# Small transfers and GpSimd arithmetic change places in a fused RWKV-7 and short-convolution kernel

## The chip, the cores and the metric

The kernel runs on one core of one Trainium2 chip. TensorE (PE in the rows) does the matrix products, VectorE (DVE) the elementwise arithmetic, ScalarE (ACT) activations, casts and copies, GpSimd (POOL) some elementwise work, and SyncE (SP) nothing but the start of transfers. Transfers can also be started from GpSimd's and ScalarE's queues; each of the five engines works through its instructions in the order in which they stand in its queue. The metric is the device time of one execution in microseconds (us), and the median of several runs.

## The reference

Two layers over 512 latent tokens with a prefix of 256 context tokens, 1024 channels, float32. Layer 0 is cut here to the part that the change touches; layer 1 is a Conformer convolution module.

```
r,k,v,za,bg,cg,xb,zb = split(h @ w_in)          # eight projections of 1024 channels
decay, a = low-rank maps of h (ev_w1, ev_w2; ev_a1, ev_a2), two directions z
kd  = k * (1 + (a - 1) * k_a)                   # two directions
S_t = S_{t-1}*decay + (S_{t-1} @ -kk)(kk*a)^T + v kd^T    # scan, 16 heads, both directions,
o_t = S_t @ r                                   # started from the state that the context leaves
bonus = sum(r * kd * r_k, per head) * v         # summed over both directions
ya  = head_group_norm(o) + bonus
yb  = bg * dwconv3(cg * xb)
y   = concat(ya * silu(za), yb * silu(zb)) @ w_out
```

## The kernel before, in words

**Number format.** A projection is a product of float32 values kept as two rounded parts, high and low. `hilo` (L121 to L128) loads a weight tile from memory into `wr..` (SyncE's queue), ScalarE casts it to the high part `wh..` (L126), and one engine subtracts to get the low part `wl..` (L127). Which engine subtracts is set by `lo_for` (L333): GpSimd for the tiles whose name begins with `bg` or `zb` (`POOL_SPLIT`, L30) and for `k0`, VectorE for the rest.

**Stages.** The 16 heads are worked on in 8 pairs of 128 channels. Layer 0 runs in 12 stages: 4 for the context chains (`c` at the end of a tile's name, two pairs each) and 8 for the latent chains (`l`, one pair each). In a latent stage `s` the program writes out, beside the chain of pair `s`: the triangular solve of the next pair (`solve`, L630 to L669), the loads, projections, decays and gates of the pair after that (`prep_lat`, `light`, `heavy`), the gates and the end of the pair's own output (`fills`, `finish`), and one of eight parts of the short convolution (`conv_branch`). A scheduler at build time decides in which order these stand in each engine's queue; the order is fixed when the kernel runs.

**The chain.** Each of its 8 steps passes the state `Hl` from VectorE (L757) to TensorE (`zol<-Hl`), on to ScalarE (`Ol` L744, `UV` L750), back to TensorE (`uh`) and to VectorE. It needs the solve of its own pair to be done.

**The solve.** It has 62 small dependent VectorE operations (L644 and L646, in turns), after a transpose of `Nt` into `X` (L638) and ahead of two transposes (L649 into `Nt`, L650 into `Y`). The end of L650 is called the end of the solve here, after which ScalarE copies (L655, L664, L669) and TensorE (`uh<-Yl`, `uh<-Nt`) finish the matrix `E` that the chain reads. `X`, `Y` and `Nt` have one buffer each; `Y` is filled from a constant in memory (`unit`, L637) ahead of every solve.

**Other lines that the change touches.** `light0` loads two small matrices `lwr` in four transfers on ScalarE's queue (L431), casts them (L434) and subtracts on GpSimd (L437). `heavy` forms `kd` (L518, then L520) and the bonus product `bon` on GpSimd (L524 to L527), followed on VectorE by the scaled products `al`, `AR`, `BK` (L528 to L544). `finish` loads the gate `gz` and stores to `ysp` (L797 to L801); `conv_branch` ends with `yb*gz` on GpSimd and a store to `ysp` (L836, L837). `psp` holds the shifted `k`, `v`, `r` and the gate `za` between a projection and its use; `h0d` holds the state that the context chains leave. `rest` (L857) loads the matrix `mod_w` in the first context stages on GpSimd's queue.

```
V.transpose(X..., Nt...)                                            # L638
for i in range(31, 0, -1):
    V.tensor_tensor(out=tv, in0=X[...], in1=Y[...], op=ALU.mult)    # L644
    V.tensor_tensor(out=Y[...], in0=Y[...], in1=tv, op=ALU.add)     # L646
```

## Time and profile before

| | |
|---|---|
| median of 3 runs | 1518.8 us (1510.12 to 1520.1) |
| the profiled execution | 1514.09 us |
| its span, first to last instruction | 1512.3 us |
| granted TensorE clock, mean of the span | 0.975 |
| span of six latent stages, 523.5 to 904.9 us | 381.4 us |

The span is 1.8 us shorter than the execution's own time. The stages of layer 0 lie between about 90 and 1000 us of it; what stands behind (output projection and layer 1) is not in the diff, apart from the low parts' engine being VectorE there already.

In the rows a line names the engine, the operation, `out<-in` tiles, the shape and a duration. A number in brackets, or behind the last bar, is how long the engine had been idle before the instruction, with what ended that idle time behind the arrow. "PEclk" is the granted TensorE clock as a share of full speed: 1.00 is 2.4 GHz and 0.50 is 1.2 GHz.

### The profile page before, as it was taken

Reading aid. Unit: us, or ns where it says so; the run is one execution under the profiler, and the core shown is the slowest. Engines: PE = TensorE matmul, PEld = TensorE weight load, DVE = VectorE, ACT = ScalarE, POOL = GpSimd, SP = SyncE. Lnnn points to the kernel's source line nnn. Section 1 sums busy time; section 2 is a strip of 40 time slices with the busy share of each in tenths; the row PEclk is TensorE's granted clock in tenths of the full one; section 3 lists DMA queues with packets and bytes.
Section 4 is the critical chain, followed back from the end, with each engine's and each line's share of the span. In section 5 each row is a group of like instructions: output and inputs, shape, how many; then the busy total and the mean of one; then the engine's idle time right before and its main releaser. Section 6 shows DMA issues by size and latency. Waiting matters only on the chain. (4 is left out here: it accounts for less than half of the span.)

```text
span 1512.3 us, 29639 instructions
## 1 busy us (share of the span) xinstructions
PE 1427.9 (94%) x11857; PEld 1015.2 (67%) x11857; DVE 991.9 (66%) x2202; ACT 745.3 (49%) x1512; POOL 205.4 (14%) x220
## 2 busy tenths in 40 slices
PE   5699999999999999999999999999999999999998
PEld 1374577878766666666666666677766676688876
DVE  2675597578788798987888987458545526444333
ACT  4323464375656566565556566447553314364322
POOL 0523200000020331322223130111100000000000
PEclk9799999999989999997999999999999999999999
DMA  8644533313232222211222222468503203033222
GB/s 308 172 140 166 159 111 100 93 55 96 74 107 68 77 70 70 71 59 58 64 66 73 71 57 63 148 219 288 179 20 112 94 19 112 28 108 98 90 95 84
DMA packets 146954, 156.59 MB, mean 104 GB/s; under 512 B 15266, under 2 KB 109154, under 8 KB 146816
## 3 DMA queue, kind: packets, MB, share of 16 engines
q1 hardware_dynamic: 134208, 128.76, 27.1%
q0 software_dynamic: 6928, 22.66, 4.5%
q10 hardware_dynamic: 5680, 3.29, 0.7%
q8 instruction: 93, 1.52, 0.4%
q14 instruction: 45, 0.37, 0.1%
HBM read 137.36 MB, written 17.31 MB: 102 GB/s over the span
## 5 line engine op out<-in xcount | busy, mean ns | idle before, releaser
L646 DVE TENSOR_TENSOR Yl<-Yl,xtmpl 128x126 f32<-128x126 f32 (+22 forms) x248 | 76.0, 306 | 4.1
L644 DVE TENSOR_TENSOR xtmpl<-Xl,Yl 128x126 f32<-128x126 f32 (+22 forms) x248 | 72.3, 292 | 4.1
L58 PE MATMUL pal<-ARl,BKl 64*128 64x128 f32 x512 | 60.4, 323 | 8.8 <-DVE E L589 6.5
L58 PEld LDWEIGHTS pal<-ARl,BKl 64*128 64x128 f32 x512 | 45.5, 211 | 26.7 <-issue 6.9
L58 PE MATMUL zol<-Hl,ARl 64*64 64x64 f32 x896 | 50.6, 232 | 9.4 <-DVE Hl L757 9.3
L589 DVE TENSOR_TENSOR E<-pal,maskE 128x512 f32<-128x512 f32 x64 | 42.3, 684 | 23.5 <-PE pal L58 17.6
L58 PE MATMUL zol<-UV,E 64*64 64x64 f32 (+1 forms) x1024 | 54.7, 223 | 0.4 <-ACT UV L750 0.4
L58 PEld LDWEIGHTS zol<-Hl,ARl 64*64 64x64 f32 x896 | 35.4, 134 | 29.3 <-issue 17.7
L62 PE MATMUL o<-wl,y 128*128 128x512 f32 x124 | 50.6, 408 | 4.2 <-DVE wl L127 4.2
L1092 DVE TENSOR_TENSOR a<-pu,a 128x512 f32<-128x512 f32 x16 | 11.1, 692 | 61.4 <-PE pu L63 59.1
L127 DVE TENSOR_TENSOR wl<-wr,wh 128x1024 fp32r<-128x1024 f32 x28 | 36.3, 1296 | 22.9 <-ACT wh L126 22.7
L61 PE MATMUL o<-wh,y 128*128 128x512 f32 x124 | 49.7, 400 | 0.0
L63 PE MATMUL o<-wh,y 128*128 128x512 f32 x124 | 49.6, 400 | 0.0
L750 ACT COPY UV<-uh 64x128 f32<-64x128 f32 x128 | 33.2, 259 | 32.7 <-PE uh L58 26.4
L1097 ACT CAST ah<-a 64x512 fp32r<-64x512 f32 x32 | 19.8, 618 | 56.0 <-DVE a L1092 55.5
L58 PEld LDWEIGHTS uh<-UV,BKt 128*64 128x64 f32 x704 | 26.5, 137 | 30.0 <-ACT UV L750 23.0
L437 POOL TENSOR_TENSOR lwll<-lwrl,lwhl 64x256 fp32r<-64x256 f32 x16 | 12.9, 808 | 243.8 <-PE pac L58 199.4
L58 PEld LDWEIGHTS zol<-UV,E 64*64 64x64 f32 (+1 forms) x1024 | 42.9, 138 | 3.4 <-ACT UV L750 2.2
L757 DVE SCALAR_TENSOR_TENSOR Hl<-uh,PCl,HPl 128x64 f32<-128x64 f32 x112 | 26.3, 276 | 27.4 <-PE uh L58 16.6
L58 PE MATMUL uh<-UV,BKt 128*64 128x64 f32 x704 | 36.5, 233 | 5.3 <-ACT UV L750 4.7
L126 ACT CAST wh<-wr 128x1024 fp32r<-128x1024 f32 x28 | 29.4, 1049 | 23.0 <-PE o L62 10.9
L58 PEld LDWEIGHTS uh<-Ol,E 64*64 64x64 f32 x512 | 20.1, 134 | 26.5 <-ACT Ol L744 18.5
(959 smaller groups left out, 4437.3 us busy)
## 6 DMA issues: line engine op xcount, KB each, us to landing
wr<-in_ev_w_out_dram SPq DMA_DIRECT2D x28, 512.0 KB, 4.0
mwr<-in_mod_w_dram POOLq DMA_DIRECT2D x32, 256.0 KB, 4.3
mwo<-in_mod_w_dram POOLq DMA_DIRECT2D x32, 256.0 KB, 3.1
ectx<-in_mod_w_dram SPq DMA_DIRECT2D x12, 512.0 KB, 4.5
wrk<-in_ev_w_in_dram SPq DMA_DIRECT2D x16, 256.0 KB, 3.0
wrv<-in_ev_w_in_dram SPq DMA_DIRECT2D x16, 256.0 KB, 2.9
wrr<-in_ev_w_in_dram SPq DMA_DIRECT2D x16, 256.0 KB, 3.1
wrza<-in_ev_w_in_dram SPq DMA_DIRECT2D x16, 256.0 KB, 3.0
```

Of the source, the lines that this page charges most:

```text
L58: return T.matmul(o, lhsT, rhs, start=start, stop=stop)
L61: T.matmul(o, ah, bh, start=start, stop=False)
L62: T.matmul(o, ah, bl, start=False, stop=False)
L63: T.matmul(o, al, bh, start=False, stop=stop)
L126: S.copy(hi, raw)
L127: env["lo"].tensor_tensor(out=lo, in0=raw, in1=hi, op=ALU.subtract)
L589: V.tensor_tensor(out=E[:, h, z * NLAT + c0 : z * NLAT + c0 + m, :], in0=pas[h], in1=maskE[:, z * (1 + h) : z * (1 + h) + 1, 0:x].to_broad ...
L644: V.tensor_tensor(out=tv, in0=X[:, :i, i : i + 1].to_broadcast([P, i, m]), in1=Y[:, i : i + 1, c0:].to_broadcast([P, i, m]), op=ALU.mult)
L646: V.tensor_tensor(out=Y[:, :i, c0:], in0=Y[:, :i, c0:], in1=tv, op=ALU.add)
L750: u_ = S.copy(UV[ZR[1 - h], i : 2 * nch - i : 2 * nch - 1 - 2 * i, ZR[h]], uh[ZR[1 - h], 0:2, :])
L757: h_ = V.scalar_tensor_tensor(out=Hn[:, z, :], in0=uh[:, 2 + z, :], scalar=PC[z][:, i : i + 1], in1=HP[:, z, :], op0=ALU.mult, op1=ALU.add)
L1097: S.copy(ahl[s][hr], a[hr])
```

## The change

GpSimd loses all its elementwise work in the latent stages and is given most of the small transfers. The low parts of `bg` and `zb` and of `lwr` and the product `yb*gz` go to VectorE. The bonus product goes to ScalarE for the first direction and to VectorE, as one fused operation and one product, for the second. The scaling of `kd` (L518) goes from VectorE to ScalarE, for latent and context pairs alike. Of the transfers, the stores and loads of `psp`, the loads of `h0d`, `gz` and `unit` and the stores to `ysp` go from SyncE's queue to GpSimd's, and the four `lwr` loads of each pair go from ScalarE's queue to GpSimd's. Line numbers of the changed kernel are one lower from L31 on.

```diff
-POOL_SPLIT = ("bg", "zb")
     def lo_for(nm):
-        env["lo"] = G if nm == "k0" or nm[:-1] in POOL_SPLIT else V
+        env["lo"] = G if nm == "k0" else V
...
-        nc.sync.dma_start(psp[p, which], rl)
+        nc.gpsimd.dma_start(psp[p, which], rl)
...
-            nc.sync.dma_start(t, psp[p, which])
+            nc.gpsimd.dma_start(t, psp[p, which])
-        nc.sync.dma_start(st["H"], h0d[p].rearrange("p (z x) -> p z x", z=2))
+        nc.gpsimd.dma_start(st["H"], h0d[p].rearrange("p (z x) -> p z x", z=2))
...
-                    nc.scalar.dma_start(raw[64 * b : 64 * b + 64, i], src[0, :, :, ps_].rearrange("z r c -> r z c"))
+                    nc.gpsimd.dma_start(raw[64 * b : 64 * b + 64, i], src[0, :, :, ps_].rearrange("z r c -> r z c"))
...
-                G.tensor_tensor(out=lwl[rows], in0=raw[rows, i], in1=lwh[rows, i], op=ALU.subtract)
+                V.tensor_tensor(out=lwl[rows], in0=raw[rows, i], in1=lwh[rows, i], op=ALU.subtract)
...
-            V.tensor_scalar(out=kd[:, cs], in0=a[:, cs], scalar1=hka[:, p : p + 1], scalar2=oka[:, p : p + 1],
-                            op0=ALU.mult, op1=ALU.add)
+            S.activation(kd[:, cs], a[:, cs], AF.Identity, scale=hka[:, p : p + 1], bias=oka[:, p : p + 1])
         V.tensor_tensor(out=kd, in0=kd, in1=k_, op=ALU.mult)
         if lat:
-            bt = w("tmp", "bt" + nm) if z else bon
-            G.tensor_scalar(out=bt, in0=kd, scalar1=col("r_k", 8 * z + p), scalar2=None, op0=ALU.mult)
+            rk = col("r_k", 8 * z + p)
             if z:
-                G.tensor_tensor(out=bon, in0=bon, in1=bt, op=ALU.add)
-                G.tensor_tensor(out=bon, in0=bon, in1=r_, op=ALU.mult)
+                V.scalar_tensor_tensor(out=bon, in0=kd, scalar=rk, in1=bon, op0=ALU.mult, op1=ALU.add)
+                V.tensor_tensor(out=bon, in0=bon, in1=r_, op=ALU.mult)
+            else:
+                S.activation(bon, kd, AF.Copy, scale=rk)
...
-        nc.sync.dma_start(Y, I["unit"])
+        nc.gpsimd.dma_start(Y, I["unit"])
...
-        G.tensor_tensor(out=yb, in0=yb, in1=gz, op=ALU.mult)
-        nc.sync.dma_start(ysp[8 + p], yb)
+        V.tensor_tensor(out=yb, in0=yb, in1=gz, op=ALU.mult)
+        nc.gpsimd.dma_start(ysp[8 + p], yb)
```

The loads of `gz`, the stores of `ysp` in `finish` and of the gate `za` change their queue in the same way. Queue by queue, SyncE goes from 420 to 321 entries and GpSimd from 203 to 254, of which 131 are transfers that were elsewhere before; VectorE goes from 2140 to 2183 and ScalarE stays at 1284.

The scheduler also puts VectorE's queue in another order. The first place is the end of a solve in the later latent stages of the kernel before, on VectorE; `Hl_4` and `Hl_5` are the states of the chain's fifth and sixth step, and `kd`, `P` and `BK` belong to the `heavy` of a later pair.

```order
L644 TENSOR_TENSOR xtmpl_8883<-Xl_8881,Yl_8882 128x16
L757 SCALAR_TENSOR_TENSOR Hl_4_8775<-uh_120,PCl_7420,HPl_4_8743 128x64
L757 SCALAR_TENSOR_TENSOR Hl_4_8775<-uh_120,PCl_7449,HPl_4_8743 128x64
L770 TENSOR_TENSOR Ol_8610<-zol_4_8751,Ol_8610 128x128
L646 TENSOR_TENSOR Yl_8882<-Yl_8882,xtmpl_8883 128x16
L518 TENSOR_SCALAR kdl_9109<-al_9100,hka,oka 128x512
L649 STREAM_TRANSPOSE Nt<-Yl_8882 128x32x16
L509 SCALAR_TENSOR_TENSOR Pl_9102<-scm,sg 128x528
L650 STREAM_TRANSPOSE Yl_8882<-Nt 128x512
L520 TENSOR_TENSOR kdl_9109<-kdl_9109,kl_9023 128x512
L757 SCALAR_TENSOR_TENSOR Hl_5_8810<-uh_120,PCl_7420,HPl_5_8778 128x64
```

The same engine and the same kind of place in the changed kernel; `wlcg` is the low part of a convolution weight, the three `bonl` rows are the end of a pair's output and the bonus of another, and `Hl_0` is the first state of the chain that this solve serves.

```order
L645 TENSOR_TENSOR Yl_8043<-Yl_8043,xtmpl_8044 128x2x15
L126 TENSOR_TENSOR wlcg_9269<-wrcg_9267,whcg_9268 128x512
L643 TENSOR_TENSOR xtmpl_8044<-Xl_8042,Yl_8043 128x16
L645 TENSOR_TENSOR Yl_8043<-Yl_8043,xtmpl_8044 128x16
L648 STREAM_TRANSPOSE Nt<-Yl_8043 128x32x16
L649 STREAM_TRANSPOSE Yl_8043<-Nt 128x512
L798 SCALAR_TENSOR_TENSOR bonl_6569<-po_8412,hcol,bonl_6569 128x512
L799 SCALAR_TENSOR_TENSOR bonl_6569<-bonl_6569,hcol,gz_8429 128x512
L623 SCALAR_TENSOR_TENSOR bonl_8223<-pbonl_8866,vl_8186 128x512
L637 STREAM_TRANSPOSE Xl_8869<-Nt 128x32x32
```

Before, the solve ends between two steps of the running chain, with the rows of the chain's last three steps still behind it; now it ends behind the running chain, three rows ahead of the next solve's transpose (L637 there), and its own chain begins right after it.

The second place is GpSimd's queue over about one latent stage, first of the kernel before.

```order
L524 TENSOR_SCALAR bonl_7404<-kdl_7422,cols_68 128x512
L127 TENSOR_TENSOR wlbg_7700<-wrbg_7698,whbg_7699 128x512
L524 TENSOR_SCALAR btl_7454<-kdl_7451,cols_68 128x512
L526 TENSOR_TENSOR bonl_7404<-bonl_7404,btl_7454 128x512
L527 TENSOR_TENSOR bonl_7404<-bonl_7404,rl_7369 128x512
L127 TENSOR_TENSOR wlbg_7706<-wrbg_7704,whbg_7705 128x512
L127 TENSOR_TENSOR wlzb_7738<-wrzb_7736,whzb_7737 128x512
L437 TENSOR_TENSOR lwll_8207<-lwrl_8201,lwhl_8206 64x256 x2
L127 TENSOR_TENSOR wlzb_7744<-wrzb_7742,whzb_7743 128x512
L836 TENSOR_TENSOR yb_7694<-yb_7694,gzb_7773 128x512
```

And of the changed kernel; `vl`, `kl`, `rl` are loads of `psp`, and `Yl<-in_unit` is the load that a solve starts from.

```order
L430 DMA lwrl_8191<-in_ev_w_dram 64x2x128
L430 DMA lwrl_8191<-in_ev_a_dram 64x2x128
L636 DMA Yl_8043<-in_unit_dram 128x512
L800 DMA ysp<-bonl_5742 128x512
L395 DMA vl_8186<-psp 128x512
L397 DMA h_4_7356<-h0d 128x128
L836 DMA ysp<-yb_7684 128x512
L395 DMA kl_9011<-psp 128x512
L395 DMA rl_9015<-psp 128x512
L796 DMA gz_8429<-psp 128x512
L430 DMA lwrl_9018<-in_ev_w_dram 64x2x128
```

Ten arithmetic operations of a stage are replaced by twelve transfers, in an order that repeats from stage to stage, each waiting for its own tile and all behind one another.

## Rows read from the trace of the kernel before

**Rows 1.** The profile's list of busy time by engine over the whole span: us, share of the span, number of instructions.

```profile
PE 1427.9 (94%) x11857; PEld 1015.2 (67%) x11857; DVE 991.9 (66%) x2202; ACT 745.3 (49%) x1512; POOL 205.4 (14%) x220
```

**Rows 2.** Busy time of each engine in windows of time, one window per latent stage; one of the six, and their sum and mean. Behind the window: its length, busy us (instructions) of each engine, and behind those the granted TensorE clock, the share of the transfer engines and GB/s.

```profile
647.20:712.90 65.70, 62.11 (x751) 42.74 (x751) 54.21 (x147) 36.96 (x88) 16.93 (x10) 0.84 0.21 63
...
sum 381.40, PE 359.49 PEld 247.53 DVE 325.02 ACT 227.51 POOL 96.54; mean PE 59.91 PEld 41.26 DVE 54.17 ACT 37.92 POOL 16.09
```

**Rows 3.** The same view of the windows between 444 and 741 us in which the granted clock was half; the two in the six latent stages, and the sum of all five.

```profile
689.80:710.20 20.40, 20.40 (x211) 14.81 (x213) 12.70 (x31) 9.04 (x16) 2.70 (x3) 0.50 0.17 50
734.10:741.00 6.90, 6.90 (x56) 4.35 (x55) 5.18 (x19) 3.84 (x10) 0.00 (x0) 0.51 0.00 0
sum 44.40, PE 44.40 PEld 32.47 DVE 30.62 ACT 19.88 POOL 7.11; mean PE 8.88 PEld 6.49 DVE 6.12 ACT 3.98 POOL 1.42
```

**Rows 4.** The timeline (start, duration, instruction, idle time before it) of VectorE, GpSimd and TensorE around 682 to 688 us, and the first and the last of 50 VectorE instructions between 398 and 960 us that lasted over 0.2 us longer than the median of their kind; the 50 together were 41.3 us longer.

```profile
429.31 0.58 DVE L413 SCALAR_TENSOR_TENSOR rnql<-rnql 128x16 f32<-128x16 f32 x1
...
682.49 0.24 DVE L644 TENSOR_TENSOR xtmpl<-Xl,Yl 128x78 f32<-128x78 f32 x1
682.63 1.77 DVE L542 TENSOR_TENSOR ARl<-rl,Pl 128x512 f32<-128x512 f32 x1
684.33 1.31 DVE L646 TENSOR_TENSOR Yl<-Yl,xtmpl 128x78 f32<-128x78 f32 x1
...
682.50 1.36 POOL L526 TENSOR_TENSOR bonl<-bonl,btl 128x512 f32<-128x512 f32 x1
683.93 1.61 POOL L527 TENSOR_TENSOR bonl<-bonl,rl 128x512 f32<-128x512 f32 x1
...
687.98 0.45 PE L58 MATMUL zol<-Hl,ARl 64*64 64x64 f32 x8 [2.02 <-DVE Hl L757]
...
953.62 1.77 DVE L827 SCALAR_TENSOR_TENSOR yb<-cx,hcol,yb 128x512 f32<-128x512 f32 x1
```

**Rows 5.** The timeline of VectorE at six marks of the latent stages: two ends of a solve (L650), the first and last state of the first latent chain and the first state of the second (L757), the end of a solve in a later stage, and the first state of the seventh chain.

```profile
514.58 0.71 DVE L650 STREAM_TRANSPOSE Yl<-Nt 128x512 f32<-128x512 f32 x1
533.68 0.24 DVE L757 SCALAR_TENSOR_TENSOR Hl<-uh,PCl,HPl 128x64 f32<-128x64 f32 x1
558.01 0.28 DVE L757 SCALAR_TENSOR_TENSOR Hl<-uh,PCl,HPl 128x64 f32<-128x64 f32 x1 [0.50 <-PE uh L58]
579.06 0.71 DVE L650 STREAM_TRANSPOSE Yl<-Nt 128x512 f32<-128x512 f32 x1
596.20 0.43 DVE L757 SCALAR_TENSOR_TENSOR Hl<-uh,PCl,HPl 128x64 f32<-128x64 f32 x2
...
752.11 0.70 DVE L650 STREAM_TRANSPOSE Yl<-Nt 128x512 f32<-128x512 f32 x1
...
921.28 0.47 DVE L757 SCALAR_TENSOR_TENSOR Hl<-uh,PCl,HPl 128x64 f32<-128x64 f32 x2
```

**Rows 6.** Groups of VectorE instructions by line over the whole span: count, busy us, mean ns of one, idle before. The last line is the same view of 964 to 1045 us.

```profile
L127 DVE TENSOR_TENSOR wlcg<-wrcg,whcg 128x512 fp32r<-128x512 f32 x16 | 10.9, 683 | 0.8 <-PE plr L63 0.8
L520 DVE TENSOR_TENSOR kdl<-kdl,kl 128x512 f32<-128x512 f32 x16 | 11.0, 685 | 0.0
L799 DVE SCALAR_TENSOR_TENSOR bonl<-po,hcol,bonl 128x512 f32<-128x512 f32 x8 | 6.0, 747 | 6.8 <-PE po L58 6.8
L518 DVE TENSOR_SCALAR kdl<-al,hka,oka 128x512 f32<-128x512 f32 x16 | 8.6, 540 | 0.0
L518 DVE TENSOR_SCALAR kdc<-ac,hka,oka 128x256 f32<-128x256 f32 x16 | 6.1, 404 | 1.0 <-ACT ac L505 0.9
...
L127 DVE TENSOR_TENSOR y<-yr,y 128x256 fp32r<-128x256 f32 x21 | 8.7, 419 | 0.0
```

**Rows 7.** Groups of ScalarE instructions by line over the whole span, with the columns of rows 6.

```profile
L354 ACT ACTIVATE lk<-plk,omu 128x512 f32<-128x512 f32 x8 | 5.4, 681 | 1.2 <-PE plk L63 1.2
L354 ACT ACTIVATE kc<-pck,omu 128x256 f32<-128x256 f32 x8 | 3.8, 474 | 6.0 <-PE pck L63 5.9
```

**Rows 8.** The timeline of ScalarE: one of the 32 starts of an `lwr` load in its queue (ACTq), and the cast that waits for a pair's four loads.

```profile
767.17 0.65 ACTq L431 DMA_DIRECT2D lwrl<-in_ev_a_dram  x1
...
769.63 0.62 ACT L434 CAST lwhl<-lwrl 128x512 fp32r<-128x512 f32 x1 [1.04 <-DMA lwrl<-in_ev_a_dram]
```

**Rows 9.** Groups of GpSimd instructions by line over the whole span, with the columns of rows 6.

```profile
L127 POOL TENSOR_TENSOR wlbg<-wrbg,whbg 128x512 fp32r<-128x512 f32 x16 | 24.8, 1551 | 57.4 <-ACT whbg L126 31.1 <-PE pcg L63 12.4 <-ACT HPl L721 11.8
L524 POOL TENSOR_SCALAR btl<-kdl,cols 128x512 f32<-128x512 f32 x8 | 18.0, 2253 | 41.9 <-DVE kdl L520 41.9
L437 POOL TENSOR_TENSOR lwll<-lwrl,lwhl 64x256 fp32r<-64x256 f32 x16 | 12.9, 808 | 243.8 <-PE pac L58 199.4 <-ACT lwhl L434 24.2 <-PE pvl L58 19.5
L857 POOL DMA_DIRECT2D mwr<-in_mod_w_dram x32 | 17.4, 546 | 12.3 <-PE mpb L58 11.6 <-PE uh L58 0.4 <-issue 0.3
```

**Rows 10.** The profile's list of transfers: tile, queue, count, KB of one, median us from its start to its landing.

```profile
mwr<-in_mod_w_dram POOLq DMA_DIRECT2D x32, 256.0 KB, 4.3
mwo<-in_mod_w_dram POOLq DMA_DIRECT2D x32, 256.0 KB, 3.1
Yc<-in_unit_dram SPq DMA_DIRECT2D x4, 256.0 KB, 3.4
wrk<-in_ev_w_in_dram SPq DMA_DIRECT2D x16, 256.0 KB, 3.0
```

**Rows 11.** TensorE's waits between 398 and 1000 us: who waited for whom, us in total, how often, the longest.

```profile
PE zol L58 <- DVE Hl L757: 9.3, 8, 2.0
```

More of the change, by code (lines that the diff above doesn't have):

```diff
@@ L796, in finish @@
         gz = w("tmp", f"gz{p}")
-        nc.sync.dma_start(gz, psp[p, 3])
+        nc.gpsimd.dma_start(gz, psp[p, 3])
         oT = st["bon"]
@@ L800, in finish @@
         V.scalar_tensor_tensor(out=oT, in0=oT, scalar=hc("lnx_b", p), in1=gz, op0=ALU.add, op1=ALU.mult)
-        (nc.gpsimd if p == 7 else nc.sync).dma_start(ysp[p], oT)
+        nc.gpsimd.dma_start(ysp[p], oT)
     def fill(p):
@@ L805, in fill @@
         gz = gate(p, 24, "za")
-        nc.sync.dma_start(psp[p, 3], gz)
+        nc.gpsimd.dma_start(psp[p, 3], gz)
     def after(anchor):
@@ L884, in fills @@
                 gz = gate(p, 24, "za")
-                nc.sync.dma_start(psp[p, 3], gz)
+                nc.gpsimd.dma_start(psp[p, 3], gz)
     sts = [prep_ctx(0, rest)]
```

## The prediction

> **What bounds the kernel now.** The list of busy time by engine comes first [rows 1]: TensorE works for 94% of the span, GpSimd for 14%. An average says little of the part that is changed, so the second view is the busy time by latent stage [rows 2]. Six stages take 381.4 us, 63.6 each; TensorE is busy for 59.9 of that, VectorE for 54.2, ScalarE for 37.9, GpSimd for 16.1. TensorE's 59.9 are not all needed. Five stretches between 444 and 741 us run at a granted clock of 0.50, the level of 1.2 GHz, with TensorE busy throughout [rows 3]: 44.4 us, of which full clock would have left at best 22.2. The longest, 20.4 us from 689.8, follows an idle time of TensorE of 2.02 us that a late `Hl` of the chain had caused [rows 4]; that stage shows 0.84 in rows 2. So layer 0 is bound by TensorE and VectorE together, and the places where one waits for the other cost twice where the clock then falls.
>
> The third view is the timeline around that idle time [rows 4]. VectorE's product into `AR` took 1.77 us, where the same shape takes 0.69 elsewhere [rows 6], and a solve operation 1.31 us, where its neighbour took 0.24. Both end about 0.5 us after a GpSimd operation that ran at the same time. All 50 stretched VectorE operations between 398 and 960 us overlap GpSimd arithmetic, none only a transfer's start on GpSimd's queue; together they are 41.3 us longer than they would be, about 5 us of every stage. VectorE's stretching is a real part of its 54.2 us.
>
> The fourth view is the marks of a stage [rows 5]. The first states of the first and seventh latent chains are (921.28 − 533.68) / 6 = 64.6 us apart: that is what a stage costs. In the first stages a solve ends late, 514.58 + 0.71 = 515.3 and 579.06 + 0.71 = 579.8, and its chain can only follow, at 533.7 and 596.2. Later it ends in mid-chain (752.8), a full chain ahead of its use.
>
> **The change, part by part.** *VectorE's arithmetic.* Added are 32 low parts at 0.683, 8 products with `gz` at 0.685, 8 fused bonus steps at 0.747 and 8 bonus products at 0.685, by the rows of those shapes [rows 6]: 21.9 + 5.5 + 6.0 + 5.5 = 38.9. The 16 `lwl` subtractions of 64x256 have no row on VectorE; between nothing and the 0.419 of 128x256 I take 0.419, 6.7 us. Removed is the scaling of `kd`, 8.6 + 6.1 [rows 6]. The stretches go with the arithmetic that they overlapped, 41.3. Net: 38.9 + 6.7 − 14.7 − 41.3 = −10.4 us over all of layer 0. In the six stages of rows 2 I put the gain at 4 us, 0.7 a stage, since the context part's scaling and the stretches ahead of the first latent stage lie outside. If only half the stretches go, VectorE has 10 us more to do, not less.
>
> *ScalarE.* Added are 16 scalings of 512 columns at 0.681, 16 of 256 at 0.474 and 8 bonus scalings at 0.681 [rows 7]: 23.9 us. Its 32 transfer starts of about 0.61 each go [rows 8]: 19.5 us. Net +4.4 us on an engine that is busy for 37.9 of 63.6 us: nothing. That cover fails where `kd` is awaited by VectorE's next product; one such wait is bounded by the 0.68 of the operation itself, 24 times 0.68, 16 us, if none were hidden. I take none, because the scheduled order sets other work between.
>
> *The queues.* GpSimd's arithmetic of 16.1 us a stage goes, and 12 transfer starts of 0.546 [rows 9], 6.5 us, come: the queue is nearly empty. SyncE's queue loses the entries that had to wait for a result, so weights wait only for their own buffers. A 256 KB load on GpSimd's queue landed 4.3 or 3.1 us after its start, on SyncE's 3.0 to 3.4 [rows 10]: up to 1.3 us later. The one load that a chain could feel is `unit` into `Y`: `Y` is free only after TensorE has read the end of the last solve, and the next solve's transpose of 2.2 us and two others' work must pass first, so that 1.3 us are covered; uncovered they would cost 8 x 1.3 = 10 us. The queue is in order, so a `ysp` store that waits for the end of a pair holds what is behind it: the loads of `v` and `h0d` and the next pair's `k`, `r`, needed about a stage later. In the context stages the `mod_w` loads stand in the same queue; between nothing and 1 us, I take nothing.
>
> From 64 such starts on GpSimd's queue (`mwr`, `mwo`), each 0.54 to 0.55 us, no VectorE operation was stretched and none of the starts was longer. The Trainium skill speaks against the change here: its page "DMA: Bandwidth & Descriptors", section "SWDGE vs HWDGE vs iDMA", says that GpSimd builds the descriptors of its transfers in on-chip memory, from which VectorE can lock it out, that queues of the other engines are immune, and its specifications put the first byte at about 1 us against 0.6. By that figure, as an estimate, eight exposed `unit` loads would cost 8 x 0.4 = 3 us; the rows' 1.3 us is the wider bound and the sum goes by that.
>
> *The order.* This is the term with the most room. In the new order every solve ends behind the running chain, three rows ahead of the next solve, and its own chain hangs on it. A stage then is one loop: end of the solve to first state, the chain, last state to the end of the next solve. The first latent stages of before ran in that way, and give prices [rows 5]. End to first state: 579.8 to 596.2, 16.4, less 0.5 of stretch, or 515.3 to 533.7, 18.4. The chain: 533.7 to 558.0, 24.3. Last state to end of the solve: 558.0 to 579.8, 21.8, of which 4.0 is stretch. The rows that stand there in VectorE's queue sum to 21.0 by their unstretched durations; in the new order such a stretch holds 29 solve rows at 0.24, 8 products `E` and 18 others at about 0.69, the two transposes of 1.1 and 0.7 and a few small rows, altogether 27.2. Scaled by (21.8 − 4.0) / 21.0 that is 23.1 us. The loop is 15.9 + 24.3 + 23.1 = 63.3; with the other first part, 18.4, it is 65.8. I take 64.0, nearer the former, which is the one that a second stage in a row of this kind showed. Against 64.6 that is −0.6 a stage, −4 us over six. Ahead of 523 us lie 12 of the 50 stretched operations, 7.9 of the 41.3 us, and 17.1 of the 44.4 us at half clock; some of both go: −3, between nothing and the 8.5 that the half clock can have cost. The forecast is −7 us on the execution's 1514.1, 1507; the median of before is 4.7 above that execution, so on its scale 1512.
>
> **The rivals.** *The stretches were the bound.* Without them the late `Hl` and the idle time ahead of it go, and with them the half clock. Of the 44.4 us, 20.4 + 6.9 = 27.3 lie in the six stages [rows 3] and cost 13.7, 2.3 a stage; 62.3 a stage gives −14, the part ahead of 523 us another −8: 1497. For it speaks that one 2.02 us idle time stands right behind two stretched operations [rows 4]; against it, that the loop above is not shorter.
>
> *The solve comes too late (slower).* If VectorE takes its rows between last state and end of solve at their plain sum of 27.2, with 18.4 ahead and 24.3 of chain, a stage is 69.9, +5.3, six times 32 us; less the 3 from ahead, 1543. It decides where last state to end of solve exceeds 64.6 − 18.4 − 24.3 = 22 us, or 24 with the shorter first part; TensorE would wait there and may fall to half clock. For it speaks that every stage of before in which the solve ended in mid-chain had slack, which is given up; against it, that the first stages of before had the late solve and were no slower.
>
> *GpSimd's queue holds the loads.* `unit`, `v`, or `lwr` late by 1.3 us each stage: 8 to 12 us, 1522.
>
> *The change does not do what it says.* If VectorE still meets GpSimd (its transfer starts stretch it as arithmetic did), the 41.3 stay and 46 − 15 = 31 us come on top; as TensorE bounds part of it, 1530.
>
> **How the numbers follow.** The forecast 0.40, the stretches as bound 0.29, the late solve 0.16, the queue 0.10, no relief 0.05. The predicted time is that of the likeliest, 1512. A change of 1%, 15 us, is about what a measurement of this kernel can tell. Faster by over 1% (under 1504) is the stretches' rival and a little of the forecast's lower side: 0.33. Slower by over 1% (above 1534) is the late solve and half of the last: 0.20, with some of the forecast's upper end. The range runs from 1490, below the stretches' rival, to 1540, into the late solve.
>
> **What would show it.** VectorE's products would be 0.69 throughout, and the 50 stretched operations gone; VectorE would be busy for 53 to 54 us a stage. The marks would be 16, 24 and 23 us. GpSimd's rows would be transfer starts of 0.54 us only. TensorE's waits for `Hl`, 9.3 us in 8 places before [rows 11], would nearly go if the stretches were the bound, and come once a stage, longer, at the first state, if the late solve rules. The prediction is wrong if the first part of the loop is far from 16 us, if the granted clock falls in every stage, or if starts on GpSimd's queue take longer than 0.55 us.

## The result, and the profile after

The changed kernel takes 1506.8 us (median of 20 runs, 1498.5 to 1520.0), the kernel before 1516.1 (20 runs, 1503.2 to 1526.0). The ratio is 0.9946, 95% interval 0.992 to 0.9972: faster by half a per cent, where 1512 against 1518.8, 0.9955, was forecast. The profiled execution took 1506.4 us with a span of 1504.6.

The same views as of before. First the busy time by engine over the span of the changed kernel, then one of its latent stages and the sum of six (545.6 to 919.0 us), to be read against [rows 1, 2].

```profile
PE 1429.3 (95%) x11857; PEld 1014.2 (67%) x11857; DVE 964.3 (64%) x2242; ACT 766.4 (51%) x1552; POOL 152.3 (10%) x263
...
672.00:733.90 61.90, 59.14 (x774) 40.12 (x773) 51.34 (x155) 39.91 (x93) 6.75 (x12) 1.00 0.24 71
...
sum 373.40, PE 356.71 PEld 242.49 DVE 309.36 ACT 241.36 POOL 36.41; mean PE 59.45 PEld 40.42 DVE 51.56 ACT 40.23 POOL 6.07
```

A stage now takes 62.2 us and every one of the six ran at full clock. GpSimd's 16 us a stage have become 6, all of them transfer starts. These windows run from the first state of one chain to that of the next, so 62.2 stands against the 64.6 of the same marks before, and not against the 63.6 of [rows 2]. Three of the six stages of before, by these marks:

```profile
533.90:596.40 62.50, 59.12 (x773) 40.71 (x771) 54.67 (x160) 38.24 (x90) 16.23 (x11) 1.00 0.24 71
659.30:731.80 72.50, 67.35 (x772) 46.63 (x772) 60.49 (x164) 38.16 (x90) 18.20 (x11) 0.86 0.20 60
860.60:921.60 61.00, 58.61 (x770) 40.63 (x770) 53.94 (x146) 38.36 (x90) 14.71 (x9) 1.00 0.23 67
```

The other three took 62.9, 66.5 (clock 0.95) and 62.3 us. The four at full clock took 62.2 on the mean, as long as the stages of the changed kernel; what the six stages lost before is the half clock in two of them.

TensorE's waits between 398 and 1000 us, of which the last answers to [rows 11]:

```profile
PE uh L57 <- ACT Ol L743: 5.4, 7, 1.0
PE pal L57 <- DVE xtmpc L643: 4.3, 1, 4.3
PE pzb L62 <- DVE wlzb L126: 3.2, 6, 0.6
PE uh L57 <- ACT UV L749: 2.8, 8, 0.6
PE zol L57 <- DVE Hl L756: 2.3, 6, 0.9
```

The waits for `Hl` fell from 9.3 to 2.3 us and the longest from 2.0 to 0.9. Summed over TensorE's timeline between 90 and 1000 us, its idle time fell from 40.1 to 29.6 us.

The half-clock windows of the changed kernel between 90 and 1000 us, against [rows 3]:

```profile
321.60:342.10 20.50, 20.44 (x151) 17.92 (x151) 6.35 (x11) 7.16 (x17) 0.17 (x1) 0.50 0.13 40
383.10:389.90 6.80, 6.80 (x63) 5.13 (x60) 6.14 (x18) 4.85 (x11) 1.59 (x3) 0.50 0.31 107
454.70:475.20 20.50, 17.44 (x200) 13.63 (x200) 10.06 (x20) 7.23 (x13) 1.08 (x2) 0.50 0.23 65
sum 47.80, PE 44.68 PEld 36.68 DVE 22.55 ACT 19.24 POOL 2.84; mean PE 14.89 PEld 12.23 DVE 7.52 ACT 6.41 POOL 0.95
```

Their sum is 47.8 us, and before it was 44.4 plus one of 3.4 at 307.5, the same; but they have moved. Before, 27.3 us of them lay in the six latent stages; now all lie in the context stages. So the profile's gain is made of two parts of opposite sign: the first state of the first latent chain comes at 545.6 us and not at 533.9, 11.7 later; from there to the last state of the last chain it takes 440.6 us and not 459.3, 18.7 less. Of the 18.7, 14.3 lie in the six stages and 4.4 in the last two chains, which ran at full clock in both profiles (67.3 us against 71.7).

The marks of a late stage, against [rows 5]: end of a solve, first and last state of the chain that hangs on it, end of the next solve.

```profile
720.19 0.71 DVE L649 STREAM_TRANSPOSE Yl<-Nt 128x512 f32<-128x512 f32 x1
733.55 0.51 DVE L756 SCALAR_TENSOR_TENSOR Hl<-uh,PCl,HPl 128x64 f32<-128x64 f32 x2
758.56 0.48 DVE L756 SCALAR_TENSOR_TENSOR Hl<-uh,PCl,HPl 128x64 f32<-128x64 f32 x2 [0.58 <-PE uh L57]
782.05 0.71 DVE L649 STREAM_TRANSPOSE Yl<-Nt 128x512 f32<-128x512 f32 x1
```

**Time and clock.** Each run lists the mean granted clock of its span: the changed kernel's 20 runs go from 0.984 at 1501.9 us to 0.966 at 1520.0, 1.2 us for each thousandth of clock. A straight line through the runs of a kernel tells its time at a given clock. At 0.975 it is 1515.0 us for 29 runs of before and 1509.3 for the 20 of the changed kernel, with 1.6 to 1.9 us of scatter about the lines. So some 6 of the 8 us are there at equal clock, and the rest is that the changed kernel is granted a little more (0.9763 against 0.9743 on the mean).

### The profile page after: what moved, and what is told of

It is laid out like the page before. It is cut to its first block, busy times and chain, and to the rows that moved or that the text cites. A ratio compares the mean times of both kernels' runs of the same rounds, so it can differ in the third digit from the quotient of the medians.

```text
span 1504.6 us, 29614 instructions
## 1 busy us (share of the span) xinstructions
PE 1429.3 (95%) x11857; PEld 1014.2 (67%) x11857; DVE 964.3 (64%) x2242; ACT 766.4 (51%) x1552; POOL 152.3 (10%) x263
## 4 chain that ended last, share of the span: by engine, by line
PE 46%; ACT 6%; DVE 5%; DMA 2%; issue 2%; DVEq 0%; SPq 0%; ACTq 0%
PE pu L61 4%; PE pu L62 4%; PE pu L60 4%; PE zol L57 3%; PE uh L57 2%; PE f L61 2%; PE f L60 2%; PE f L62 2%; PE pz L61 2%; PE pz L62 2%; PE pz L60 2%; PE px L57 2%; PE pc L57 1%; PE pal L57 1%; PE o L62 1%
## 5 line engine op out<-in xcount | busy, mean ns | idle before, releaser
L645 DVE TENSOR_TENSOR Yl<-Yl,xtmpl 128x126 f32<-128x126 f32 (+22 forms) x248 | 62.5, 252 | 2.2
L643 DVE TENSOR_TENSOR xtmpl<-Xl,Yl 128x126 f32<-128x126 f32 (+22 forms) x248 | 62.4, 252 | 2.0
L126 DVE TENSOR_TENSOR wl<-wr,wh 128x1024 fp32r<-128x1024 f32 x28 | 37.1, 1323 | 20.7 <-ACT wh L125 20.5
L588 DVE TENSOR_TENSOR E<-pal,maskE 128x512 f32<-128x512 f32 x64 | 43.5, 685 | 10.4 <-PE pal L57 10.2
L125 ACT CAST whcg<-wrcg 128x512 fp32r<-128x512 f32 x16 | 9.9, 621 | 63.5 <-DMA wrcg<-in_ev_w_in_dram 51.2
L125 ACT CAST wh<-wr 128x1024 fp32r<-128x1024 f32 x28 | 29.4, 1051 | 21.4 <-PE o L61 11.9
```

Source lines behind the costliest of these rows:

```text
L125: S.copy(hi, raw)
L126: env["lo"].tensor_tensor(out=lo, in0=raw, in1=hi, op=ALU.subtract)
L588: V.tensor_tensor(out=E[:, h, z * NLAT + c0 : z * NLAT + c0 + m, :], in0=pas[h], in1=maskE[:, z * (1 + h) : z * (1 + h) + 1, 0:x].to_broad ...
L643: V.tensor_tensor(out=tv, in0=X[:, :i, i : i + 1].to_broadcast([P, i, m]), in1=Y[:, i : i + 1, c0:].to_broadcast([P, i, m]), op=ALU.mult)
L645: V.tensor_tensor(out=Y[:, :i, c0:], in0=Y[:, :i, c0:], in1=tv, op=ALU.add)
```

## The experiments

Theory A: GpSimd's arithmetic stretched VectorE, TensorE waited for that, and this is what was gained. Rival B: it is SyncE's freed queue. Rival C: only the clock differed, by chance.

Each experiment was measured beside runs of the kernel before of its own, whose medians lie between 1511.9 and 1516.9 us, so two experiments are compared by their ratios; 0.001 is 1.5 us. The scheduler also works anew for each build. By the traces only e4 and e8 keep the order of VectorE's, ScalarE's and TensorE's instructions of the kernel that they were made from, and e5 nearly does. What any other run gains or loses belongs to its edit together with the order that it brings.

**Each half alone.** e1 puts the transfers of the changed kernel back on their old queues; e2 moves the transfers in the kernel before and leaves its arithmetic.

```diff
 # e1, from the changed kernel; likewise every other moved transfer
-        nc.gpsimd.dma_start(psp[p, which], rl)
+        nc.sync.dma_start(psp[p, which], rl)
...
 # e2, from the kernel before; likewise every other moved transfer
-        nc.sync.dma_start(psp[p, which], rl)
+        nc.gpsimd.dma_start(psp[p, which], rl)
```

> The arithmetic of the change alone; all transfers stay on the queues of the kernel before. Theory A (GpSimd's arithmetic stretched VectorE, and the gain is that this is over): no VectorE operation of the latent stages over 0.2 us longer than its median, TensorE idle between 90 and 1000 us near the 29.6 of the changed kernel and not the 40.1 of before, ratio to before 0.992 to 0.997. Rival B (the gain is SyncE's queue, freed of entries that wait): ratio 0.998 to 1.002, TensorE's idle time near 40. Rival C (only the granted clock differs by chance): at equal mean granted clock the time is that of before, within 2 us.

Measured: 1506.3 us, ratio 0.9934 (0.9907 to 0.996); no VectorE operation stretched between 398 and 960 us; TensorE's idle time between 90 and 1000 us 25.4.

> The queues of the change alone; all arithmetic stays where it was before, so GpSimd does both its arithmetic (16 us a stage) and 12 transfer starts a stage. Theory A: the stretches stay at about 41 us in all between 398 and 960 us, ratio 0.998 to 1.004, and slower if transfers stand behind arithmetic in GpSimd's queue. Rival B: ratio 0.992 to 0.997. Rival C: at equal mean granted clock the time is that of before, within 2 us.

Measured: 1520.5 us, ratio 1.001 (0.998 to 1.004); 54 stretched operations, 47.1 us in all; TensorE's idle time 40.9. Its wait for `Hl` and its half clock in the latent stages:

```profile
PE zol L58 <- DVE Hl L757: 7.3, 8, 1.6
...
580.90:594.50 13.60, 13.60 (x217) 11.08 (x216) 4.61 (x6) 9.80 (x17) 1.14 (x2) 0.50 0.13 41
632.10:635.50 3.40, 3.40 (x28) 1.91 (x28) 2.27 (x8) 1.41 (x4) 1.29 (x3) 0.50 0.67 215
761.80:785.70 23.90, 23.76 (x191) 17.00 (x193) 11.72 (x26) 8.83 (x17) 7.85 (x11) 0.50 0.16 47
```

The whole gain is in the arithmetic; the queues alone give nothing. B falls. So does C: at a clock of 0.975 the line through e1's runs stands at 1506.9 us and that of before at 1515.0.

**One queue term by itself.** e4 changes one line, and all other engines keep their order.

```diff
-        nc.gpsimd.dma_start(Y, I["unit"])
+        nc.sync.dma_start(Y, I["unit"])
```

> The changed kernel with the load of the unit matrix (12 transfers) back on SyncE's queue; the order of all other instructions is the same. The forecast (the load is covered): no change, within 3 us of the changed kernel's 1507. Rival (GpSimd's queue holds the load): 8 to 12 us faster than the changed kernel, 1495 to 1499.

Measured: 1506.3 us, ratio 0.9941 (0.9915 to 0.9968), the changed kernel's time. The load is covered on either queue. Its profile also shows how much of one profile is chance: with the same order of work the first latent state came at 539.4 us, not 545.6, because the 20.5 us of half clock at 321.6 were absent.

**Bringing GpSimd's arithmetic back.** Three ways. e3 and e5 let GpSimd do the subtractions for `bg` and `zb` a second time, e3 in the changed kernel, e5 in e1; e6 gives them back to GpSimd instead of VectorE.

```diff
 # e3 and e5: behind VectorE's subtraction in hilo, for the tiles of bg and zb
+        G.tensor_tensor(out=raw, in0=raw, in1=hi, op=ALU.subtract)   # the test for these tiles is left out here
...
 # e6, from the changed kernel
-        env["lo"] = G if nm == "k0" else V
+        env["lo"] = G if nm == "k0" or nm[:-1] in ("bg", "zb") else V
```

> The changed kernel, in which GpSimd does the 32 subtractions for bg and zb a second time, into the raw weight tile that nobody reads any more. Theory A: 25 to 30 us of VectorE stretching come back, and the time goes up by 4 to 8 us against the changed kernel, to 1511 to 1515. If the gain is the new order of VectorE's queue (solves that end behind the chain in every stage) and not the missing stretches, the time stays at 1507 within 3 us, since the order in that respect is the same.

Measured: 1532.3 us, ratio 1.012 (1.0079 to 1.0161), 26 us above the changed kernel by the ratios and far more than expected, with 20.2 us of stretching. GpSimd's queue also holds the transfer starts behind this arithmetic, and VectorE's order is not the same; e5 leaves the transfers out.

> The arithmetic of the change alone, as in e1, and GpSimd does the 32 subtractions for bg and zb a second time, into the raw weight tile that nobody reads any more. GpSimd's queue holds no transfers here in the latent stages, and VectorE's, TensorE's and ScalarE's queues stand in nearly the order of e1, so this adds GpSimd's arithmetic beside VectorE and nothing else but a raw tile held some 2 us longer. Theory A: some 20 us of stretching come back, TensorE's idle time between 90 and 1000 us goes from 25 to 33 us or more, the time goes from e1's 1506 to 1512 to 1520. If the missing stretches are not what gains: 1504 to 1509. If e3's 26 us came from transfers standing behind arithmetic in GpSimd's queue, this run shows much less of it, 1508 to 1512.

Measured: 1522.5 us, ratio 1.009 (1.0055 to 1.0126), 24 us above e1 by the ratios; 20.6 us of stretching; TensorE's idle time 33.9 us. It looks like theory A, but the trace tells otherwise. In five stages in a row TensorE is idle for 1.6 to 2.0 us at one place, and 3.4 us of half clock follow. One of them, on TensorE and ScalarE:

```profile
651.75 0.27 PE L563 MATMUL pbl<-ident,BKl 64*128 64x64 f32 x1 [1.74 <-ACT BKt L599]
...
650.59 0.62 ACT L125 CAST whzb<-wrzb 128x512 fp32r<-128x512 f32 x1 [9.47 <-DMA wrzb<-in_ev_w_in_dram]
...
652.70:656.10 3.40, 3.40 (x35) 2.54 (x36) 3.26 (x13) 1.07 (x2) 0.65 (x1) 0.50 0.41 119
```

The copy `BKt` stands in ScalarE's queue behind the cast of a weight tile, and that tile came late. The waits of SyncE's queue say why: its weight load waits for the raw buffer that GpSimd now gives back.

```profile
SPq L122 <- POOL wrbg L127: 121.6, 12, 20.2
...
SPq L122 <- POOL wrzb L127: 21.8, 12, 2.9
```

So a raw tile "held some 2 us longer", which the expectation had put aside, is what costs here. 1.7 us of idle time, and 3.4 us at half clock, worth as much again, cover the 2.8 us by which a stage of e5 (64.7) is longer than one of e1 (61.9); nothing is left for the stretching itself. e5 does not show theory A, and e3, which has the same tile held, doesn't either.

> The changed kernel with the 32 subtractions for bg and zb back on GpSimd, instead of VectorE: VectorE has 21.9 us less to do by itself, and meets GpSimd's arithmetic again. Theory A (contention costs VectorE about as much as the work itself, and at moments that nobody chose): VectorE's busy time in the latent stages within 10 us of the changed kernel's, the time 1508 to 1516. If the added work were what matters, VectorE being short of time: faster than the changed kernel by 4 us or more, under 1503.

Measured: 1515.3 us, ratio 1.0024 (0.9989 to 1.0059), 12 us above the changed kernel by the ratios, in A's range, and VectorE's busy time in the six stages is 311.7 us against 309.4, as A has it. But again the loss is not where A has it. 27.3 us of stretching are back, and the six latent stages take 61.7 us each, no more than in the changed kernel. Two windows of it, then TensorE's longest waits between 90 and 1000 us:

```profile
679.10:740.40 61.30, 59.56 (x774) 40.16 (x773) 51.12 (x151) 40.06 (x93) 13.82 (x16) 1.00 0.24 70
740.40:802.50 62.10, 59.65 (x774) 40.36 (x773) 52.51 (x150) 40.12 (x93) 12.38 (x16) 1.00 0.24 71
...
PE pal L57 <- DVE xtmpc L643: 4.3, 1, 4.3
PE pal L57 <- DVE Yl L645: 4.2, 1, 4.2
```

The loss lies ahead of the first latent chain, whose first state comes at 554.8 us and not at 545.6, and in the last two chains (71.2 us against 67.3). Of the two waits, at 453 and 525 us, the first stands in the changed kernel too; the second is new, and 13.7 us of half clock begin at its end. In this order of work stretching costs the six stages nothing. That makes a rival D: the new order of VectorE's queue, with a solve that always ends behind the chain, brought the gain.

**Short arithmetic in the old order.** e8 decides between A and D. In the kernel before, GpSimd's operations are cut to 8 columns, and the order of VectorE's, TensorE's and ScalarE's queues stays word for word.

```diff
 # e8, from the kernel before; the same cut for bt, bon (three operations) and yb
-        env["lo"].tensor_tensor(out=lo, in0=raw, in1=hi, op=ALU.subtract)
+        q = slice(0, 8) if env.get("cut") and raw.shape[-1] == 512 else slice(None)
+        env["lo"].tensor_tensor(out=lo[:, q], in0=raw[:, q], in1=hi[:, q], op=ALU.subtract)
...
-            mm3(o, wh[:, ks], wl[:, ks], ...)
+            mm3(o, wh[:, ks], wl[:, 0:1].to_broadcast([P, P]) if cut else wl[:, ks], ...)
```

> The kernel before with GpSimd's arithmetic for bg, zb, the bonus and yb cut to 8 of 512 columns, and what reads the low parts and the bonus reading those columns over and over. Left out of the computation: 504 of 512 columns of those products, so the output is another. The order of VectorE's, TensorE's and ScalarE's queues is exactly that of before, with the solves that end in mid-chain, and so is the work of these three engines; only GpSimd's operations are short. Theory A (the stretches of VectorE put TensorE idle and the clock at half): the stretches fall from 41 us to under 8, TensorE's waits for Hl go below 4 us, the six latent stages come to 62.5 us or less each, the time is 1500 to 1508 where before takes 1512 to 1516. Rival D (the new order of VectorE's queue brought the gain, and stretching costs nothing, as 27 us of it in e6 left the latent stages at 61.7 us): the stages stay at 64 to 66 us with half clock in them, and the time is that of before within 3 us.

Measured: 1481.4 us, ratio 0.9785 (0.9744 to 0.9826), 33 us faster than before and 19 us under A's range. Five stretched operations, 2.3 us, are left, all beside the subtraction of `lwl`, which was not cut. One stage, the sum of six (529.5 to 892.1 us), and the wait for `Hl`:

```profile
712.10:771.70 59.60, 58.41 (x771) 41.09 (x772) 49.93 (x145) 38.05 (x90) 4.95 (x11) 1.00 0.25 73
...
sum 362.60, PE 354.72 PEld 245.47 DVE 305.77 ACT 229.56 POOL 28.80; mean PE 59.12 PEld 40.91 DVE 50.96 ACT 38.26 POOL 4.80
...
PE zol L58 <- DVE Hl L757: 0.5, 2, 0.3
```

A stage takes 60.4 us, TensorE's idle time in layer 0 halves from 40.1 to 20.0 us, and of 27.3 us at half clock in the latent stages 3.4 are left. D falls: the old order without the long GpSimd operations is faster than the new order. In the order of before, GpSimd's arithmetic cost 33 us.

The run alone doesn't part the stretching from the raw weight tiles that GpSimd held until its own subtraction was done. TensorE's idle times in the kernel before do, as far as one trace can. Of those over 0.3 us between 523.5 and 960 us, 14, 14.4 us together, wait for VectorE and end within 2 us behind a stretched operation, as the 2.02 us of [rows 4] does. Three, 3.3 us together, wait for the copy `Ol`, which stood in ScalarE's queue behind a cast whose tile came late. This is the cast ahead of the longest, 1.6 us at 794 us:

```profile
792.77 0.62 ACT L126 CAST whxb<-wrxb 128x512 fp32r<-128x512 f32 x1 [2.56 <-DMA wrxb<-in_ev_w_in_dram]
```

Ahead of this one a load had started only as GpSimd's subtraction ended (786.6 us); ahead of the other two the late load waited for VectorE. In e8, from 523.5 us on, no idle time over 0.3 us stands within 2 us behind a stretched operation and none waits for that copy, while TensorE's waits for `UV` are as they were (4.7 us). So most of the idle time that went stood behind the stretching, and the held tiles show in one place.

**What the change paid back.** If the arithmetic on GpSimd cost 33 us, the change should have gained far more than 8. e10 cuts the operations that it gave VectorE, in the changed kernel, in the manner of e8.

```diff
 # e10, from the changed kernel; the subtraction and the matmul as in e8
-                V.scalar_tensor_tensor(out=bon, in0=kd, scalar=rk, in1=bon, op0=ALU.mult, op1=ALU.add)
-                V.tensor_tensor(out=bon, in0=bon, in1=r_, op=ALU.mult)
+                V.scalar_tensor_tensor(out=bon[:, 0:8], in0=kd[:, 0:8], scalar=rk, in1=bon[:, 0:8], ...)
+                V.tensor_tensor(out=bon[:, 0:8], in0=bon[:, 0:8], in1=r_[:, 0:8], op=ALU.mult)
```

> The changed kernel with the operations for bg, zb, the second bonus direction and yb cut to 8 of 512 columns, on VectorE where the change put them. Left out of the computation: 504 of 512 columns of those products, so the output is another. VectorE does 39 us less than in the changed kernel, and the scheduler, which counts its time, lets the solves of the later stages end in mid-chain again. If the added work on VectorE, with the late solves that it brings, is what the change pays back: 1478 to 1488, that of e8, with stages of 60 to 61 us. If the new queues or kd's scaling on ScalarE pay back a part: 1490 to 1505.

Measured: 1490.8 us, ratio 0.985 (0.9796 to 0.9904), at the lower end of the second case. The late solves end in mid-chain again and a stage takes 60.2 us, as in e8 (60.4). So VectorE's added work, with the late solves that the scheduler makes of it, pays back about 15 us (0.985 to 0.9946). Added work and late solves were not parted: the scheduler counts VectorE's time, so the one brings the other. Whatever else parts e10 from e8 pays back about 10 more (0.9785 to 0.985): the queues, `kd` and the first bonus direction on ScalarE, the uncut `lwl` on VectorE, and its own order. By their intervals both figures are uncertain by 9 to 10 us. In the profiles most of the second lies ahead of the first latent chain, whose first state comes at 534.3 us against 529.5 in e8, with 17.1 us of half clock from 321 us.

**The move of kd.** e7 puts `kd`'s scaling back on VectorE in the changed kernel, e9 in e1, e11 in e1 for the context pairs alone, and e12 in e1 for the latent pairs alone.

```diff
 # e7 from the changed kernel, e9 from e1; in e11 "if not lat", in e12 "if lat"
-            S.activation(kd[:, cs], a[:, cs], AF.Identity, scale=hka[:, p : p + 1], bias=oka[:, p : p + 1])
+            V.tensor_scalar(out=kd[:, cs], in0=a[:, cs], scalar1=hka[:, p : p + 1], scalar2=oka[:, p : p + 1],
+                            op0=ALU.mult, op1=ALU.add)
```

> The changed kernel with the scaling of kd back on VectorE: 14.7 us more on VectorE, 18.5 us less on ScalarE. If VectorE's time is what bounds the latent stages: 1512 to 1518. If TensorE bounds them now (it is busy for 59 of 62 us a stage in the changed kernel) and VectorE has room: 1505 to 1510.

Measured: 1497.1 us, ratio 0.9912 (0.9883 to 0.994): under both cases. By the ratios it is 5 us faster than the changed kernel, with intervals that overlap. VectorE has room.

> The arithmetic of the change without its move of kd's scaling, and the transfers on the queues of before: the two parts of the change that the runs so far show to gain nothing are undone. If they gain nothing or cost something together: 1492 to 1500, at or under e7. If the queues do help where VectorE is fuller: 1500 to 1508.

Measured: 1495.9 us, ratio 0.9873 (0.9826 to 0.992). It has the lowest ratio of the kernels that do the whole computation, 1.3% faster than before: the arithmetic off GpSimd, `kd` on VectorE, the queues as they were. By the ratios that is 9 us under e1; e7 and e11 lie inside its interval.

> As e1 (the arithmetic of the change alone, queues of before), with kd's scaling of the context pairs alone back on VectorE; that of the latent pairs stays on ScalarE. If the move of kd costs in the context stages (TensorE waits 0.9 us for a ScalarE copy there, and 20 us of half clock follow in e1 and in the changed kernel): 1494 to 1499, that of e9. If it costs in the latent stages: 1503 to 1508, that of e1.

Measured: 1498.2 us, ratio 0.9888 (0.9853 to 0.9923), 7 us under e1 and near e9.

> As e1, with kd's scaling of the latent pairs alone back on VectorE; that of the context pairs stays on ScalarE. If the move costs in the context stages: 1503 to 1508, that of e1. If in the latent stages: 1494 to 1499, that of e9.

Measured: 1513.5 us, ratio 0.9978 (0.9941 to 1.0015), in neither case: 7 us above e1 and 16 above e9.

The context pairs' scaling is what costs: on ScalarE it is 7 us dearer where the latent pairs' is there too (e1 against e11) and 16 where that is on VectorE (e12 against e9), each with the order that comes with it. The latent pairs' scaling costs nothing on ScalarE (e11 against e9, 2 us). In all eight traces with the context scaling on ScalarE, TensorE is idle there for 1.2 us and for 0.9 us, waiting for ScalarE at two places; in the other six these two are not there, but three or four waits of 0.65 to 0.70 us for ScalarE's `ac` are. The half clock between 90 and 400 us comes to 6.8 to 30.7 us in the eight, and to 0 to 10.2 in the six. The two waits in the changed kernel come first; behind them stands the window from 90 to 400 us, of e1 and then of e11.

```profile
226.76 0.50 PE L60 MATMUL plr<-hlh,whr 128*128 128x512 f32 x1 [1.20 <-ACT whr L125]
...
320.44 0.27 PE L563 MATMUL pbc<-ident,BKc 64*128 64x64 f32 x1 [0.92 <-ACT BKt L599]
```

```profile
90.00:400.00 310.00, 305.05 (x2429) 219.79 (x2429) 203.46 (x486) 150.37 (x304) 25.13 (x47) 0.95 0.34 105
```

```profile
90.00:400.00 310.00, 302.52 (x2633) 218.71 (x2627) 217.22 (x521) 154.56 (x315) 25.14 (x47) 1.00 0.35 108
```

In the same 310 us e1 gets through 2429 matrix products with the clock at 0.95, e11 through 2633 at 1.00. The half clock of the context stages (20.5 us from 322 us in e1, 20.5 from 227 us in e12) follows one wait or the other; in e7 and e11 there is none before 400 us, in e9 one of 10.2 us.

## Why the prediction was right, and where its steps were not

The time, its sign and the range held. The sum that gave it did so by errors that cancelled: −4 for the six stages and −3 ahead of them were forecast, −7 together; the profiles have −14.3 and +11.7, −4.4 in the last two chains, for which the sum had no term, and −0.7 behind them, −7.7 together. That the totals agree is luck.

**What bounds.** "TensorE and VectorE together" was half right. The 64.6 us of a stage of before hold 27.3 / 6 = 4.5 us at half clock, of which full clock would have left half: 62.3. The changed kernel's stages take 62.2 at full clock, with TensorE busy for 59.5, and the stages of before that ran at full clock took as long. TensorE bounds; VectorE matters by where it makes TensorE wait.

**VectorE's arithmetic: right.** Its new rows cost what the rows of those shapes said, the low parts within 2 ns and the one without a row (64x256) at the upper bound, and all 50 stretched operations are gone:

```profile
L126 DVE TENSOR_TENSOR wlbg<-wrbg,whbg 128x512 fp32r<-128x512 f32 x16 | 11.0, 685 | 0.0
...
L436 DVE TENSOR_TENSOR lwll<-lwrl,lwhl 64x256 fp32r<-64x256 f32 x16 | 6.7, 416 | 0.3
...
L523 DVE SCALAR_TENSOR_TENSOR bonl<-kdl,cols,bonl 128x512 f32<-128x512 f32 x8 | 6.0, 746 | 0.0
```

The durations of all VectorE instructions sum to 1084.9 us against 1096.8, −11.9 where −10.4 was worked out, and VectorE is busy for 51.6 us a stage, where 53 to 54 were named. What the step missed is that a sum of VectorE's time is no time of the kernel. With 41 us of stretching, GpSimd's arithmetic cost 33 in the order of before (e8), and the 27 of e6 cost its six stages nothing. One reading was off: of the two stretched operations in [rows 4] only the first ended 0.5 us behind GpSimd's; the second, a small solve operation, ended 0.1 us behind.

**ScalarE, "+4.4 us: nothing": wrong.** The price was low, and the cover was only looked up in the latent stages.

```profile
L517 ACT ACTIVATE kdl<-al,oka,hka 128x512 f32<-128x512 f32 x16 | 13.1, 816 | 0.1
L517 ACT ACTIVATE kdc<-ac,oka,hka 128x256 f32<-128x256 f32 x16 | 9.3, 593 | 0.0
```

An operation with a scale and a bias by column took 816 and 593 ns, not 681 and 474. The step that failed is the wait put at nothing. Its bound of 16 us counted the 24 latent operations alone, and the cost came from the 16 of the context pairs: e11, which undoes the move for these, gains 7 us on e1, e9 and e7, which undo it for all, 9 and 5.

**The queues: right.** e2 and e4 show no effect. The `unit` load landed in 3.4 us from GpSimd's queue, and VectorE was not stretched by a start:

```profile
Yl<-in_unit_dram POOLq DMA_DIRECT2D x8, 256.0 KB, 3.4
...
L636 POOL DMA_DIRECT2D Yl<-in_unit_dram x7 | 4.0, 567 | 122.8 <-PE uh L57 122.8
L430 POOL DMA_DIRECT2D lwrl<-in_ev_w_dram x12 | 7.2, 602 | 12.5 <-ACT osq L785 5.9 <-DVE kkl L474 5.8 <-DVE BKl L543 0.8
```

The starts of 128x512 tiles took 0.54 to 0.57 us on the mean of a group, beside a VectorE that was busy for 51 of 62 us. Those of `lwr` took 0.60, by whichever cause; with these, and with 0.567 for `unit`, the sign of over 0.55 us that the text named came up, without a cost that a run shows. (Of the 64 starts that it took its price from, one had lasted 0.71.) The Trainium skill, in the section "SWDGE vs HWDGE vs iDMA" of its page "DMA: Bandwidth & Descriptors", warns that VectorE, in what it calls 2-port perf mode, locks GpSimd out of the memory into which it writes the descriptors. The traces don't show in which mode VectorE ran; no such loss is seen in these rows.

**The order, "the term with the most room": mis-sized.** The loop came out as 720.90 to 733.55, 733.55 to 758.56 and 758.56 to 782.76: 12.7, 25.0 and 24.2 us, 61.9 in all, where 15.9, 24.3 and 23.1 were put and 64.0 taken. The first part is the one that failed, and a first part far from 16 us was a sign of being wrong that the text named. It was read from two stages of before, in which TensorE and ScalarE had other work queued ahead of what the solve's end releases: in the second, TensorE ran products for `pzb` from 585.8 to 590.6 us. VectorE is not even what the loop hangs on: it stands idle at the solve's end until TensorE has made `pbonl`, in seven stages 22.9 us together:

```profile
DVE bonl L623 <- PE pbonl L57: 22.9, 7, 4.0
```

So six stages gave −14.3 us in the profiles and not −4, and nearly all of that is clock: 27.3 us at half clock, worth 13.7, are gone, and the order by itself gave nothing at full clock.

**Ahead of the first latent stage, −3: wrong sign.** It came out at +11.7 in the profiles, with 47.8 us at half clock up to the first state against 20.5. Part goes with ScalarE's waits, part is chance, as e4 shows with 30.7 us for the same order.

**The rivals.** The stretches as bound had the right mechanism: the 62.3 us a stage that it priced were met, and e8 shows GpSimd's arithmetic to cost even more than it said. Its total of 1497 failed on the same context stages. The late solve did not cost what was feared: TensorE's longest wait for `Hl` is 0.9 us. Its 1543 was counted from the profiled execution; on the scale of the median, as the other times are, it is 1548. By the runs the half per cent is 33 us gained by taking GpSimd's arithmetic away, about 15 paid back as work on VectorE with the order it brings, and about 10 in the rest, of which undoing the move of `kd` gives back 5 to 9.

## What to carry to other kernels

Price an engine's arithmetic by what it does to the engine beside it, and at the moments where a third engine waits: here GpSimd's 16 us of arithmetic a stage, for which no wait of TensorE between 398 and 1000 us stands in the trace, cost 33 in all. When work is moved off, look where it lands in every stage, the lightly read ones too: a scaling moved to ScalarE was free in the latent stages and cost some 7 to 16 us in the context stages. And undo a change's parts one by one before it is kept whole: this one without the move of `kd` and of the queues gained 1.3%, the whole 0.5%.

## What the runs showed of the hardware

The changed kernel's 20 runs spread over 21 us and lie on a line with the granted clock, with 1.6 us of scatter, so that two kernels can be compared at equal clock. An idle time of TensorE can be followed by half clock in one execution and not in the next, with the order of work the same: after 0.9 us at 320 us the changed kernel has 20.5 us of half clock, and e4 none. A start on GpSimd's queue leaves VectorE alone: of the changed kernel's 177 starts between 90 and 1000 us 134 overlapped a VectorE operation, and none of these was over 0.2 us longer than the median of its kind. GpSimd's arithmetic does not: of 255 VectorE operations that overlapped it between 398 and 960 us in the kernel before, 50 were that much longer, and 47 of these ended shortly behind a GpSimd operation, those of 128x512 by 0.55 us, where they take 0.69 alone, and the small ones by 0.02 to 0.16 us.
